# A hybrid SSD and MLA decode step: splitting the MLA output weight in an earlier stage and keeping its halves in DRAM

## The chip, the cores and the metric

The kernel runs on one core of one Trainium2 chip. The metric is the device time of one execution in microseconds, the median of several runs. The profile is that of one more execution.

## What is computed

The reference is a two-layer model: a Mamba-2 SSD mixer, then a multi-head latent attention (MLA) mixer, each behind an RMS norm and added to the residual, and a final RMS norm. A prompt of 1024 tokens and a sample group of 8 x 8 tokens go through the same weights. The sample group attends to 16 cached pages of 128 rows for each of its 8 sequences. The part that matters here is the end of the MLA layer:

```python
def mla_sample_attn(q_nope, q_pe, ckv, kpe, pool_ckv, pool_kpe, layer, page_table, w_uk, w_uv):
    q_lat = absorb(q_nope, w_uk)
    stats = latent_partial(q_lat, q_pe, ckv, kpe, causal)
    def page_step(carry, pt):
        page = latent_partial(q_lat, q_pe, pool_ckv[layer, pt], pool_kpe[layer, pt], None)
        return merge_partial(carry, page), None
    (_, l, acc), _ = lax.scan(page_step, stats, page_table.T)
    return latent_out(l, acc, w_uv)

def mla_output(o, gate, w_out):
    gated = o.reshape(b, t, MLA_WIDTH) * jax.nn.silu(gate.astype(F32))
    return jnp.einsum('bte,ed->btd', gated.astype(gate.dtype), w_out)
```

`w_out` is a float32 matrix of 1024 x 1024.

## The kernel before

Products are made from float32 operands in halves: ScalarE rounds an operand to the matmul's format (the high half), VectorE or GpSimd subtracts it from the original (the low half), and three products hi x hi, hi x lo and lo x hi are summed in PSUM. `split` is the helper. So a weight is loaded raw, cast, subtracted, and only then used.

The kernel is one program in stages. `layer_ssd` is the first layer. `mla_in` normalises, then computes the gates (`gate_block` for eight blocks of 128 columns, three pieces of tokens each; blocks 0 and 1 run inside the norm, blocks 2 to 7 as the generator `gates`), then the key-value latents (`mla_kv`, nine tiles of tokens) and the query latents (`mla_cq`). `mla_q` and `mla_heads` make the prompt's attention head by head. Inside the last head the sample group's work begins, as the generator `flow`; `mla_sample` drains the rest of it.

`flow` goes over 32 "pages": page n is an item of 512 cached rows of one sequence. A page transposes the rows of the next (`turn`, `ct`), transposes its predecessor's probabilities (`turn_p`, `pt`), makes seven score products (`scores`, `sc`), the softmax on VectorE and ScalarE (`weigh`), and twelve value products for its predecessor (`values`, `o`). Every fourth page starts a sequence with its new rows (`first_scores`, `first_values`, `first_acc`). Cached rows come by indirect loads on GpSimd's queue, four pages ahead (`load`); the rotary rows of two pages at a time come by three loads on SP's queue (`load_tk`, tile `tk`, two buffers).

Into the same pages the prompt's output projection is woven (`MlaOut.pieces`): each `next(out.fill)` is twelve products of a tile of 128 tokens with the output weight. The pieces begin at page 8 (`OUT0`), and some pages take two (`MORE`). A tile needs its attention rows (`og` from `og_d`), split into `oh` and `ol`, and its residual `h`.

The output weight has eight slices of 128 rows, in the order `WORD`. Two are loaded raw in the last head (`preload`, into `w5p`), six at the start of `mla_sample` and after (`weight`, into the three buffers that later hold `h`, named `w5r`). Pages 2 to 7 split them (`WSP` gives the page of each): one cast of 128 x 1024 on ScalarE (`w5h`), four subtractions of 128 x 256 (`w5l`) on GpSimd or VectorE in turn (`WENG`), pinned behind the page's own work by `issue_after`.

The order on TensorE and GpSimd is written out by hand in the heads and the sample stage. On ScalarE, VectorE and SP's queue a planner sorts the instructions by when they are expected to be ready; `issue_after` forces an order there. SP's queue is in order: an instruction that waits for a buffer or a result holds all behind it.

Of the kernel before, what the change touches and what calls it, by code (L numbers as in the profile page):

```python
# [51 lines left out]
MORE = (10, 12, 14, 18)  # L52
WSP = (2, 3, 4, 4, 5, 6, 6, 7)
WENG = (2, 0, 2, 0, 2, 0, 2, 0)
WORD = (0, 4, 6, 1, 2, 3, 5, 7)
# [260 lines left out]
def load_w(k, pool, src, nk, ncol, tag, bufs=3, raws=None, rbufs=2, eng=None, sub=0, late=None):  # L316
    raw = load_raw(raws or pool, nk, ncol, rbufs)
    k.nc.sync.dma_start(raw, src.rearrange("(k p) e -> p k e", p=128))
    hi = pool.tile([128, nk, ncol], F32R, tag=tag + "h", name=tag + "h", bufs=bufs)
    lo = pool.tile([128, nk, ncol], F32R, tag=tag + "l", name=tag + "l", bufs=bufs)  # L320
    if late is None:
        split(k, hi, lo, raw, eng, sub)
    else:
        late.append((hi, lo, raw))
    return hi, lo
# [635 lines left out]


def gate_block(k, wp, raws, b):
    ws = kslices(load_w(k, wp, k.I["mla_w_in"][0][:, 800 + 128 * b : 928 + 128 * b], 8, 128, "wg", 3, raws, eng=k.nc.gpsimd, sub=4), 8)
    gt = wp.tile([128, T], F32, tag="gt", name=f"gt{b}", bufs=2)

    def ev(ci, t0, n, p):
        k.nc.scalar.activation(gt[:, t0 : t0 + n], p[:, :n], AF.Silu)

    for ci in range(3):  # L970
        proj_piece(k, k.psum, ws, k.xh, k.xl, ci, ev)
        yield
    k.nc.sync.dma_start(k.g_d[b], gt)
# [13 lines left out]
def mla_in(k, right, mid):  # L987
    tc, nc, I = k.tc, k.nc, k.I
    k.g_d = k.dram.tile([8, 128, T], F32, name="g_d")
    with ExitStack() as st:  # L990
# [3 lines left out]

        rw = st.enter_context(open_pool(tc, name="rw", bufs=1))
        sg = ExitStack()
        wg = sg.enter_context(open_pool(tc, name="wpg", bufs=1))
# [8 lines left out]
        k.kvs = [k.cm.tile([128, 2, 64], F32R, name=f"kvs{x}") for x in "hl"]  # L1006
        gates = (None for b in range(2, 8) for _ in gate_block(k, wg, rw, b))
        with open_pool(tc, name="kg", bufs=1, side="right") as kg:
# [20 lines left out]
        wcq = load_cw(k, wq, rw, 0, 512, "cw")  # L1029
        mla_kv(k, sp, wkv)  # L1030
        wk.close()
# [5 lines left out]

def mla_kv(k, sp, ws):
    nc, I = k.nc, k.I
# [7 lines left out]
    for i, (t0, m) in enumerate(TILES):  # L1047
# [39 lines left out]
        if i < 8:  # L1087
            kh, kl = k.kT
            split(k, kh[64:96, t0 : t0 + m], kl[64:96, t0 : t0 + m], p[64:96, 256 : 256 + m])


# [363 lines left out]
def mla_heads(k, hd, sm, early, st):  # L1455
# [8 lines left out]
    for h in range(MH):  # L1464
# [19 lines left out]
        for t in range(12):  # L1484
            qc, jb = (0, t) if t < 4 else (1, t - 4)
            held.append((h, qc, jb, *hd.qk(h, qc, jb)))
            if t == 0:
                step(turn)
                turn = b
            while done < total * (t + 1) // 12:  # L1490
                step(units[done])
                done += 1
            if h + 1 == MH and t == 0:
                sm.preload()
            if len(held) > LEAD:
                hd.pv(*held.pop(0))
# [44 lines left out]
class Sample:  # L1541
# [28 lines left out]

    def preload(self):
        k = self.k
        self.pre = ExitStack()
        pp = self.pre.enter_context(open_pool(k.tc, name="pre4", bufs=1))
        self.wraw = {}
        for kk in WORD[:2]:
            self.wraw[kk] = pp.tile([128, D], F32, name=f"w5p{kk}")
            with k.tc.issue_after(k.lastq.ins):
                k.nc.sync.dma_start(self.wraw[kk], k.I["mla_w_out"][0][kk * 128 : kk * 128 + 128])

# [15 lines left out]
    def late_open(self, st):  # L1596
        self.pre.close()
# [10 lines left out]
    def load_tk(self, n):  # L1608
        k, nc = self.k, self.k.nc
        tk = self.ep.tile([96, 4, 256], F32R, tag="tk", name=f"tk{n}", bufs=2)  # L1610
        for j in range(3):
            src = k.kpe_d[j % 2][:, :, 128 * n : 128 * n + 256].rearrange("r c x -> c r x")
            with k.tc.issue_after(k.lastq.ins):
                nc.sync.dma_start(tk[32 * j : 32 * j + 32].bitcast(F32), src)
        for j in range(2):
            self.tk[n + j] = tk[:, :, 128 * j : 128 * j + 128]
# [12 lines left out]
    def softmax(self, name, s, n, old):  # L1629
# [4 lines left out]
        if old is None:  # L1634
            nc.vector.tensor_scalar(nm, mx, -SCALE, None, op0=ALU.mult)
        else:
            self.nmi = nc.vector.tensor_scalar(nm, mx, -SCALE, old, op0=ALU.mult, op1=ALU.min)
        P = self.sp.tile([128, n], F32, tag=f"P4{n}", name=f"P4{name}", bufs=2)
# [42 lines left out]
    def turn(self, n, c):  # L1681
# [6 lines left out]
        tl = self.ep.tile([128, 512], F32R, tag=f"cTl{c}", name=f"cTl{n}_{c}", bufs=2)  # L1688
        a = nc.scalar.copy(th, pt)
        b = nc.vector.tensor_tensor(tl, pt, th.bitcast(F32), op=ALU.subtract)  # L1690
        if self.out:
            self.out.pins = a, b
        self.cT[n, c] = (th, tl)
# [85 lines left out]
    def flow(self):  # L1779
        N = len(self.items)  # L1780
        for n in range(-1, N + 1):
# [9 lines left out]
            if t:  # L1791
                self.turn(n + 1, 1)
                yield
            parts = [WORD[WSP.index(n) + x] for x in range(WSP.count(n))] if out else []
            for kk in parts:
                out.weight_split(kk, 0)
            if 0 <= n < N:
                self.scores(n)
                self.weigh(n)
            if parts:  # L1800
                out.pins = out.pins[0], self.nmi
            for kk in parts:
                out.weight_split(kk, 1)
            if n % 4 == 3 and t:
# [19 lines left out]
            if out:  # L1824
                if n in MORE:
                    next(out.fill, None)
                if n + 1 == OUT0[0]:
                    next(out.fill)
                    self.k.nc.sync.dma_start(out.fw, self.k.I["final_norm_w"].partition_broadcast(128))
            yield  # L1830


def mla_sample(k, sm, flow):
    with ExitStack() as st:
        psum = st.enter_context(open_pool(k.tc, name="ps4", bufs=1, space=PS))
        out = MlaOut(k, st, psum)
        sm.open(st, psum, out)
        out.raw = sm.wraw
        for kk in WORD[2:5]:
            out.weight(kk)  # L1840
        out.fill = fill = out.pieces(range(8))
        next(fill)
        for _ in flow:
            if not hasattr(sm, "accT") and not any(kk in out.raw for kk in WORD[:2]):
                sm.late_open(st)
        last = None
# [11 lines left out]
class MlaOut:  # L1858
    def __init__(self, k, st, psum):
        tc, nc, I = k.tc, k.nc, k.I  # L1860
# [3 lines left out]
        self.fw = sp.tile([128, D], F32, name="fw")  # L1864
        self.raw = {}
        self.ws = [[self.wp.tile([128, D], F32R, name=f"w5{x}{kk}", bufs=1) for x in "hl"] for kk in range(8)]

    def weight(self, kk):
        k, nc, wp = self.k, self.k.nc, self.wp
        self.raw[kk] = self.sp.tile([128, D], F32, tag="h5", name=f"w5r{kk}", bufs=3)  # L1870
        WQ(nc).dma_start(self.raw[kk], k.I["mla_w_out"][0][kk * 128 : kk * 128 + 128])

    def weight_split(self, kk, half):
        hi, lo = self.ws[kk]
        raw = self.raw[kk]
        nc, x = self.k.nc, WENG[WORD.index(kk)]
        if not half:
            with self.k.tc.issue_after(self.pins[0].ins):
                nc.scalar.copy(hi, raw)
        for a in range(2 * half, 2 * half + 2):  # L1880
            s = slice(256 * a, 256 * a + 256)
            with self.k.tc.issue_after(self.pins[1].ins):
                (nc.gpsimd if x & 2 else nc.vector).tensor_tensor(lo[:, s], raw[:, s], hi[:, s].bitcast(F32),
                                                                  op=ALU.subtract)
        if half:
            del self.raw[kk]
            if 2 <= WORD.index(kk) < 5:
                self.weight(WORD[WORD.index(kk) + 3])

    def pieces(self, tiles, src=None):  # L1890
        k, nc, sp, ws = self.k, self.k.nc, self.sp, self.ws

        def load(i):
# [4 lines left out]
            if i < 8:  # L1898
                g = sp.tile([128, 8, 128], F32, tag="og5", name=f"og5{i}", bufs=2)
                nc.sync.dma_start(g, k.og_d[:, :, t0 : t0 + m].rearrange("b p t -> p b t"))  # L1900
            return oh[:, :, :m], oh[:, :, 64:] if m == 64 else ol, g, oh
# [7 lines left out]
        for n, i in enumerate(tiles):  # L1909
            t0, m = TILES[i]  # L1910
            oh, ol, _, o2 = queue.pop(0)
            h = sp.tile([128, D], F32, tag="h5", name=f"h5{i}", bufs=3)
            nc.sync.dma_start(h[:m], k.h_d[t0 : t0 + m])
            if n + 1 < len(tiles):
# [5 lines left out]
            for hf, c in enumerate(cs):  # L1920
# [3 lines left out]
                for j, _ in enumerate(mm_tok(nc, p, m, nw, [  # L1924
                        (oh[:, kk], ol[:, kk], o2[:, kk], ws[kk][0][:, c], ws[kk][1][:, c]) for kk in WORD])):
                    if j == (7 if src else 11) and nw == 512:
# [138 lines left out]
```

## Time and profile before

| what | value |
|---|---|
| median of 3 runs | 1947.31 us (1943.63 to 1948.73) |
| profiled execution | 1942.63 us |
| its span, first to last instruction | 1940.9 us |
| granted TensorE clock, mean | 0.995 |
| busy share PE, DVE, ACT, POOL | 98%, 61%, 57%, 44% |
| DMA moved | 202.02 MB, mean 104 GB/s |

PE is TensorE's products, DVE is VectorE, ACT is ScalarE, POOL is GpSimd; a trailing q means the engine's sequencer or queue (SPq issues most of the DMAs). Times are microseconds from the start of the span. A row of a timeline has start, length, engine, source line, operation, `out<-in`, shapes, and in brackets how long the engine stood idle before it and who released it. In the table by windows come, for each stretch, its length, the busy time of each engine with its instructions in brackets, the granted clock as a share of full speed, the busy share of the DMA engines and GB/s.

### The profile page before, as it was taken

The page shows a single profiled execution, that of the slowest core. Times are in us where ns is not written, and L with a number is a line of the kernel's source. Part 1 is how long each engine was busy: PE and PEld are TensorE (multiplying, and loading weights), DVE is VectorE, ACT ScalarE, POOL GpSimd, SP SyncE. Part 2 cuts the span into 40 slices and gives each one's busy share as a digit, 9 for nine tenths or more (in the row PEclk, how much of TensorE's full clock was granted, in tenths as well). Part 3 has the DMA queues.
Part 4 walks back from the last instruction along what each step waited for, and adds up shares of the span by engine and source line. Part 5 has one row for each costly group of instructions (what it writes and reads, how often), then busy time and mean ns, then how long its engine had stood idle before and what let it go on. Part 6 is the DMA issues. An engine that isn't in the chain of part 4 may idle for free.

```text
span 1940.9 us, 33581 instructions
## 1 busy us (share of the span) xinstructions
PE 1896.4 (98%) x12023; PEld 1731.9 (89%) x12023; DVE 1191.3 (61%) x2447; ACT 1110.6 (57%) x2535; POOL 844.3 (44%) x1122
## 2 busy tenths in 40 slices
PE   9999999999999999899999999999999999999998
PEld 7999999999999999788787998898888888778887
DVE  5557565756665666765533104466787878676674
ACT  6466676666667676743214314335777777855552
POOL 2447455555655555444003213203443434774551
PEclk9999999999999999999999999999999999999999
DMA  5123323332333332553533333132111112654441
GB/s 165 50 72 87 92 84 98 82 110 82 93 89 93 83 99 66 189 180 133 197 124 109 134 141 91 64 109 89 55 52 41 52 41 59 205 177 154 155 128 39
DMA packets 181087, 202.02 MB, mean 104 GB/s; under 512 B 18828, under 2 KB 147608, under 8 KB 180536
## 3 DMA queue, kind: packets, MB, share of 16 engines
q1 hardware_dynamic: 175864, 180.08, 30.3%
q0 software_dynamic: 4976, 19.66, 3.0%
q8 instruction: 95, 1.56, 0.3%
q14 instruction: 72, 0.59, 0.1%
q10 hardware_dynamic: 80, 0.13, 0.0%
HBM read 146.52 MB, written 53.28 MB: 103 GB/s over the span
## 4 chain that ended last, share of the span: by engine, by line
PE 85%; ACT 4%; DVE 3%; DMA 3%; POOL 2%; issue 1%; SPq 0%; POOLq 0%; DVEq 0%; ACTq 0%
PE pj L86 21%; PE pz L98 8%; PE pq L98 6%; PE pob L98 5%; PE p L98 5%; PE poa L98 5%; PE py L635 2%; PE sc L86 2%; PE o L86 2%; PE sc L1365 2%; PE o L1428 2%; PE o L1430 2%; PE st L1397 2%; PE st L1398 2%; PE st L1399 2%; PE o L1429 2%
## 5 line engine op out<-in xcount | busy, mean ns | idle before, releaser
L86 PE MATMUL pj<-xh,wih 128*128 128x384 f32 (+1 forms) x768 | 254.7, 336 | 0.5 <-ACT raw L512 0.3
L86 PE MATMUL pj<-xl,wih 128*128 128x384 f32 (+1 forms) x768 | 254.1, 331 | 0.0
L86 PE MATMUL pj<-xh,wil 128*128 128x384 f32 (+1 forms) x768 | 253.6, 330 | 0.0
L1411 POOL TENSOR_TENSOR tl<-P,th 128x384 fp32r<-128x384 f32 (+1 forms) x96 | 90.6, 944 | 232.5 <-ACT P L1409 190.9
L526 DVE SCALAR_TENSOR_TENSOR acc<-raw,vec,acc 128x1112 f32<-128x1112 f32 x96 | 141.6, 1476 | 26.5 <-ACT acc L522 25.5
L86 PEld LDWEIGHTS pj<-xh,wih 128*128 128x128 f32 x768 | 144.3, 189 | 2.2 <-ACT xh L273 0.7
L86 PEld LDWEIGHTS pj<-xl,wih 128*128 128x128 f32 x768 | 144.9, 189 | 1.0
L86 PEld LDWEIGHTS pj<-xh,wil 128*128 128x128 f32 x768 | 144.7, 188 | 0.4
L98 PE MATMUL pz<-wih,xh 128*128 128x256 f32 x504 | 142.8, 287 | 0.5 <-ACT z L567 0.5
L98 PE MATMUL pz<-wil,xh 128*128 128x256 f32 (+1 forms) x504 | 140.2, 284 | 0.0
L1408 ACT ACTIVATE th<-st 128x512 fp32r<-128x512 f32 x192 | 94.6, 493 | 65.9 <-PE st L1404 50.3
L98 PE MATMUL pz<-wih,xl 128*128 128x256 f32 x448 | 128.2, 286 | 0.0
L630 ACT ACTIVATE M<-M,tok 128x128 f32<-128x128 f32 (+1 forms) x288 | 90.9, 386 | 64.2 <-DVE M L627 63.8
L1701 POOL TENSOR_TENSOR kvl<-pgr,kvh 128x256 fp32r<-128x256 f32 x128 | 97.6, 789 | 57.4 <-ACT kvh L1699 57.0
L98 PEld LDWEIGHTS pz<-wih,xh 128*128 128x128 f32 x504 | 95.9, 190 | 1.3 <-ACT z L567 0.9
L1409 ACT ACTIVATE P<-st 128x512 f32<-128x512 f32 x192 | 93.5, 487 | 0.0
L98 PEld LDWEIGHTS pz<-wil,xh 128*128 128x128 f32 (+1 forms) x504 | 92.7, 184 | 0.7
L627 DVE TENSOR_TENSOR M<-M,negu 128x512 f32<-128x512 f32 x64 | 50.6, 790 | 67.2 <-DMA M<-acs_d 67.1
L133 DVE TENSOR_TENSOR wil<-wraw,wih 128x512 fp32r<-128x512 f32 x88 | 72.2, 828 | 25.8 <-ACT wih L127 22.7
L98 PEld LDWEIGHTS pz<-wih,xl 128*128 128x128 f32 x448 | 85.3, 190 | 0.1
L613 POOL TENSOR_TENSOR xdd<-xsT,tok 128x256 f32<-128x256 f32 x64 | 50.2, 784 | 80.7 <-ACT xsT L599 80.3
L1411 DVE TENSOR_TENSOR tl<-P,th 128x512 fp32r<-128x512 f32 x96 | 70.8, 737 | 18.9 <-ACT P L1409 18.0
(832 smaller groups left out, 6308.3 us busy)
## 6 DMA issues: line engine op xcount, KB each, us to landing
wraw<-in_ssd_w_in SPq DMA_DIRECT2D x92, 256.0 KB
M<-acs_d SPq DMA_DIRECT2D x64, 256.0 KB
s<-in_state_ssm SPq DMA_DIRECT2D x32, 256.0 KB
y_d<-y SPq DMA_DIRECT2D x64, 128.0 KB
out_s_ssm<-s SPq DMA_DIRECT2D x32, 256.0 KB
wraw<-in_ssd_w_out SPq DMA_DIRECT2D x12, 512.0 KB
q_d<-qt SPq DMA_DIRECT2D x32, 192.0 KB
qp<-q_d SPq DMA_DIRECT2D x8, 768.0 KB
```

Of the source, the lines that this page charges most:

```text
L86: nc.tensor.matmul(out, a, b, start=(i == 0), stop=(i == n - 1))
L98: nc.tensor.matmul(o, a, b, start=(j == 0), stop=(j == len(ops) - 1))
L133: return (eng or nc.vector).tensor_tensor(lo, src, hi.bitcast(F32), op=ALU.subtract)
L526: last = nc.vector.scalar_tensor_tensor(acc, raw[:, j : j + n], k.convw[j][:, blk : blk + 1], acc, op0=ALU.mult, op1=ALU.add)
L613: nc.gpsimd.tensor_tensor(v3(xdd), v3(xsT), hb(2), op=ALU.mult)
L627: nc.vector.tensor_tensor(M[:m, :, :m], M[:m, :, :m], (k.negs if smp else k.negu)[:m, :m].unsqueeze(1).to_broadcast([m, 4, m]), op=ALU.add)
L630: nc.scalar.activation(M[:m, h, :m], M[:m, h, :m], AF.Exp, bias=tk[:, 0, 4 * g + h : 4 * g + h + 1])
L635: nc.tensor.matmul(py[:m, h * 64 : h * 64 + 64], M[:m, h, :m], xsT[:m, h * 64 : h * 64 + 64], start=True, stop=True)
L1408: nc.scalar.activation(th[:, :n], ps[:, :n], AF.Exp, scale=SCALE)
L1409: nc.scalar.activation(P[:, :n], ps[:, :n], AF.Exp, scale=SCALE)
L1411: eng.tensor_tensor(tl[:, :n], P[:, :n], th[:, :n].bitcast(F32), op=ALU.subtract)
L1701: nc.gpsimd.tensor_tensor(rl[:, j], raw[:, j], rh[:, j].bitcast(F32), op=ALU.subtract)
```

## The change

The output weight's split leaves the pages. A generator `stage_out` handles it in sixteen steps of half a slice (128 x 512): load raw, cast on ScalarE, subtract in place on VectorE, store both halves to a DRAM tensor `w5_d`. Nine of the steps are taken among the pieces of gate blocks 2 to 7, the rest behind the latent tiles of `mla_kv`. Each raw load is put behind the newest weight load of `load_w`.

In the last head `preload` fetches two slices in halves (1 MB each) that stay where they are; pages 2 to 7 fetch one slice each, put behind the newest rotary-row load on SP's queue. The loads of attention rows, residuals and the final norm's weight are put behind the newest rotary rows too. The first attention tile is loaded at page 6 and split at page 7; before, its load was asked for at the start of `mla_sample`. The accumulator tiles of `late_open` no longer wait for the preloaded slices' memory.

```diff
-WSP = (2, 3, 4, 4, 5, 6, 6, 7)
-WENG = (2, 0, 2, 0, 2, 0, 2, 0)
+NPW = 2
+WSP = (2, 3, 4, 5, 6, 7)
@@ load_w
-    k.nc.sync.dma_start(raw, src.rearrange("(k p) e -> p k e", p=128))
+    k.lastload = k.nc.sync.dma_start(raw, src.rearrange("(k p) e -> p k e", p=128))
@@
+def stage_out(k, pool):
+    nc = k.nc
+    k.w5_d = k.dram.tile([8, 128, 2, D], F32, name="w5_d")
+    for n in range(16):
+        kk, s = WORD[n // 2], slice(512 * (n % 2), 512 * (n % 2) + 512)
+        t = pool.tile([128, 2, 512], F32, tag="w5s", name=f"w5s{n}", bufs=3)
+        with k.tc.issue_after(k.lastload.ins):
+            nc.sync.dma_start(t[:, 1], k.I["mla_w_out"][0][kk * 128 : kk * 128 + 128, s])
+        nc.scalar.copy(t[:, 0].bitcast(F32R), t[:, 1])
+        nc.vector.tensor_tensor(t[:, 1].bitcast(F32R), t[:, 1], t[:, 0], op=ALU.subtract)
+        nc.sync.dma_start(k.w5_d[kk][:, :, s], t)
+        yield
@@ mla_in
         rw = st.enter_context(open_pool(tc, name="rw", bufs=1))
+        stage = stage_out(k, st.enter_context(open_pool(tc, name="w5s", bufs=1)))
...
-        gates = (None for b in range(2, 8) for _ in gate_block(k, wg, rw, b))
+        def gate_steps():
+            for b in range(2, 8):
+                for ci, _ in enumerate(gate_block(k, wg, rw, b)):
+                    if (3 * b + ci) % 2:
+                        next(stage, None)
+                    yield
+        gates = gate_steps()
...
-        mla_kv(k, sp, wkv)
+        mla_kv(k, sp, wkv, stage)
@@ mla_kv, at the end of each tile
+        next(stage, None)
@@ Sample.preload
-        for kk in WORD[:2]:
-            self.wraw[kk] = pp.tile([128, D], F32, name=f"w5p{kk}")
+        for kk in WORD[:NPW]:
+            self.ws[kk] = pp.tile([128, 2, D], F32R, name=f"w5{kk}")
             with k.tc.issue_after(k.lastq.ins):
-                k.nc.sync.dma_start(self.wraw[kk], k.I["mla_w_out"][0][kk * 128 : kk * 128 + 128])
+                k.nc.sync.dma_start(self.ws[kk].bitcast(F32), k.w5_d[kk])
@@ Sample.load_tk
-                nc.sync.dma_start(tk[32 * j : 32 * j + 32].bitcast(F32), src)
+                self.lasttk = nc.sync.dma_start(tk[32 * j : 32 * j + 32].bitcast(F32), src)
@@ Sample.flow
-            parts = [WORD[WSP.index(n) + x] for x in range(WSP.count(n))] if out else []
-            for kk in parts:
-                out.weight_split(kk, 0)
+            if out and n >= 0:
+                out.weights(n)
             if 0 <= n < N:
                 self.scores(n)
                 self.weigh(n)
-            if parts:
-                out.pins = out.pins[0], self.nmi
-            for kk in parts:
-                out.weight_split(kk, 1)
...
+                if n + 2 == OUT0[0]:
+                    next(out.fill)
                 if n + 1 == OUT0[0]:
                     next(out.fill)
-                    self.k.nc.sync.dma_start(out.fw, self.k.I["final_norm_w"].partition_broadcast(128))
+                    with self.k.tc.issue_after(self.lasttk.ins):
+                        self.k.nc.sync.dma_start(out.fw, self.k.I["final_norm_w"].partition_broadcast(128))
@@ mla_sample
         sm.open(st, psum, out)
-        out.raw = sm.wraw
-        for kk in WORD[2:5]:
-            out.weight(kk)
+        sm.late_open(st)
+        k.sm = sm
         out.fill = fill = out.pieces(range(8))
-        next(fill)
...
@@ MlaOut
+    def weights(self, n):
+        k = self.k
+        for x in range(WSP.count(n)):
+            kk = WORD[NPW + WSP.index(n) + x]
+            with k.tc.issue_after(k.sm.lasttk.ins):
+                WQ(k.nc).dma_start(self.ws[kk].bitcast(F32), k.w5_d[kk])
@@ MlaOut.pieces
-                nc.sync.dma_start(g, k.og_d[:, :, t0 : t0 + m].rearrange("b p t -> p b t"))
+                with k.tc.issue_after(k.sm.lasttk.ins):
+                    nc.sync.dma_start(g, k.og_d[:, :, t0 : t0 + m].rearrange("b p t -> p b t"))
...
-            nc.sync.dma_start(h[:m], k.h_d[t0 : t0 + m])
+            with k.tc.issue_after(k.sm.lasttk.ins):
+                nc.sync.dma_start(h[:m], k.h_d[t0 : t0 + m])
```

More of the change, by code (lines that the diff above doesn't have):

```diff
@@ L1035, in mla_in, with mla_kv @@
         mla_cq(k, sp, wcq)
-def mla_kv(k, sp, ws):
+def mla_kv(k, sp, ws, stage):
     nc, I = k.nc, k.I
@@ L1493, in mla_heads @@
             if h + 1 == MH and t == 0:
-                sm.preload()
+                sm.preload(st)
             if len(held) > LEAD:
@@ L1569, in pt, with preload @@
         return self.psum.tile([128, 512], F32, tag=tag, name=name, bufs=bufs)
-    def preload(self):
+    def preload(self, st):
         k = self.k
-        self.pre = ExitStack()
-        pp = self.pre.enter_context(open_pool(k.tc, name="pre4", bufs=1))
-        self.wraw = {}
-        for kk in WORD[:2]:
-            self.wraw[kk] = pp.tile([128, D], F32, name=f"w5p{kk}")
+        pp = st.enter_context(open_pool(k.tc, name="pre4", bufs=1))
+        self.ws = {}
+        for kk in WORD[:NPW]:
+            self.ws[kk] = pp.tile([128, 2, D], F32R, name=f"w5{kk}")
             with k.tc.issue_after(k.lastq.ins):
-                k.nc.sync.dma_start(self.wraw[kk], k.I["mla_w_out"][0][kk * 128 : kk * 128 + 128])
+                k.nc.sync.dma_start(self.ws[kk].bitcast(F32), k.w5_d[kk])
     def load_cn(self, b):
@@ L1596, in late_open @@
     def late_open(self, st):
-        self.pre.close()
         ap = st.enter_context(open_pool(self.k.tc, name="ap4", bufs=1))
@@ L1636, in softmax @@
         else:
-            self.nmi = nc.vector.tensor_scalar(nm, mx, -SCALE, old, op0=ALU.mult, op1=ALU.min)
+            nc.vector.tensor_scalar(nm, mx, -SCALE, old, op0=ALU.mult, op1=ALU.min)
         P = self.sp.tile([128, n], F32, tag=f"P4{n}", name=f"P4{name}", bufs=2)
@@ L1688, in turn @@
         tl = self.ep.tile([128, 512], F32R, tag=f"cTl{c}", name=f"cTl{n}_{c}", bufs=2)
[L1689 to L1692, printed above, removed]
+        split(k, th, tl, pt)
         self.cT[n, c] = (th, tl)
@@ L1835, in mla_sample @@
         psum = st.enter_context(open_pool(k.tc, name="ps4", bufs=1, space=PS))
-        out = MlaOut(k, st, psum)
+        out = MlaOut(k, st, psum, sm)
         sm.open(st, psum, out)
-        out.raw = sm.wraw
-        for kk in WORD[2:5]:
-            out.weight(kk)
+        sm.late_open(st)
+        k.sm = sm
         out.fill = fill = out.pieces(range(8))
-        next(fill)
-        for _ in flow:
-            if not hasattr(sm, "accT") and not any(kk in out.raw for kk in WORD[:2]):
-                sm.late_open(st)
+        drain(flow)
         last = None
@@ L1858, with __init__ @@
 class MlaOut:
-    def __init__(self, k, st, psum):
+    def __init__(self, k, st, psum, sm):
         tc, nc, I = k.tc, k.nc, k.I
@@ L1864, in __init__ @@
         self.fw = sp.tile([128, D], F32, name="fw")
[L1865 to L1888, printed above, removed]
+        self.ws = dict(sm.ws)
+        for kk in WORD[NPW:]:
+            self.ws[kk] = self.wp.tile([128, 2, D], F32R, name=f"w5{kk}", bufs=1)
+    def weights(self, n):
[4 more added lines that the diff above has]
+                WQ(k.nc).dma_start(self.ws[kk].bitcast(F32), k.w5_d[kk])
     def pieces(self, tiles, src=None):
@@ L1924, in pieces @@
                 for j, _ in enumerate(mm_tok(nc, p, m, nw, [
-                        (oh[:, kk], ol[:, kk], o2[:, kk], ws[kk][0][:, c], ws[kk][1][:, c]) for kk in WORD])):
+                        (oh[:, kk], ol[:, kk], o2[:, kk], ws[kk][:, 0, c], ws[kk][:, 1, c]) for kk in WORD])):
                     if j == (7 if src else 11) and nw == 512:
```

## The prediction, made before the changed kernel was run

> **What bounds the kernel now.** I read the page first (PE is busy for 98% of the span, and the chain that ended last is 85% PE), so time can only come from stretches in which PE is not full. The table by windows finds the one that the change touches.
>
> ```profile
> core 0: us, PE busy (x) PEld busy (x) DVE busy (x) ACT busy (x) POOL busy (x), PEclk, DMA share, GB/s
> 1081.86:1158.25 76.39, 75.22 (x468) 74.79 (x468) 5.44 (x8) 17.54 (x33) 15.99 (x23) 1.00 0.36 131
> 1158.25:1197.20 38.95, 38.95 (x270) 36.99 (x269) 14.56 (x78) 13.18 (x40) 15.44 (x24) 1.00 0.30 88
> 1653.00:1660.00 7.00, 7.00 (x48) 6.28 (x47) 4.26 (x9) 6.57 (x17) 5.64 (x7) 1.00 0.96 321
> 1675.25:1718.69 43.44, 34.91 (x209) 29.72 (x207) 38.42 (x74) 30.86 (x57) 36.25 (x45) 0.88 0.81 251
> 1679.50:1693.50 14.00, 9.54 (x60) 8.37 (x61) 11.26 (x25) 11.88 (x22) 8.58 (x11) 0.90 1.01 307
> 1690.00:1700.00 10.00, 7.91 (x30) 6.65 (x31) 10.00 (x17) 8.39 (x16) 6.83 (x8) 0.54 0.94 272
> 1718.69:1907.00 188.31, 188.31 (x1117) 163.03 (x1116) 118.86 (x262) 101.65 (x221) 98.37 (x124) 1.00 0.42 135
> ```
>
> The stretch 1675.25 to 1718.69 holds the sample pages 2 to 7, where the output weight is split today. PE is busy for 34.91 of 43.44 us and DVE for 38.42. From page 8 on the output pieces fill PE (188.31 of 188.31 us): what those pages take is PE's own work, and the change leaves it alone. So the question is how much sooner page 8 starts. The timeline of PE gives each page's first score product, and the wait list of PE for the same stretch says what held it.
>
> ```profile
> 1675.25 0.48 PE L86 MATMUL sc<-cTh,qlh 128*128 128x512 f32 x1
> 1680.60 0.48 PE L86 MATMUL sc<-cTh,qlh 128*128 128x512 f32 x1
> 1686.97 0.48 PE L86 MATMUL sc<-cTh,qlh 128*128 128x512 f32 x1
> 1698.58 0.78 PE L86 MATMUL sc<-cTh,qlh 128*128 128x512 f32 x1
> 1705.72 0.48 PE L86 MATMUL sc<-cTh,qlh 128*128 128x512 f32 x1
> 1712.38 0.48 PE L86 MATMUL sc<-cTh,qlh 128*128 128x512 f32 x1
> 1718.69 0.48 PE L86 MATMUL sc<-cTh,qlh 128*128 128x512 f32 x1
> 1720.43 0.48 PE L98 MATMUL p<-w5h,oh 128*128 128x512 f32 x1
> ```
>
> ```profile
> engine line waited for: us in total, times, longest us
> PE pt L1728 <- ACT P L1640: 3.5, 4, 1.9
> PE pt41n L1667 <- ACT P41n L1640: 3.2, 1, 3.2
> PE o L86 <- DVE pTl L133: 1.7, 2, 1.0
> ```
>
> The page periods are 5.35, 6.37, 11.61, 7.14, 6.66 and 6.31 us. PE never waits for a DMA here: it waits 8.4 us in all for ACT and DVE, most of it for the softmax. Why those were late shows in their timelines:
>
> ```profile
> 1684.32 0.16 DVE L1659 TENSOR_TENSOR sn<-sc41n,smk 128x8 f32<-128x8 f32 x1
> 1685.11 3.86 DVE L1883 TENSOR_TENSOR w5l<-w5p,w5h 128x256 fp32r<-128x256 f32 x4
> 1688.89 0.15 DVE L1632 TENSOR_REDUCE mx41n<-sn 128x1 f32<-128x8 f32 x1
> ...
> 1689.74 2.00 ACT L1879 CAST w5h<-w5r 128x1024 fp32r<-128x1024 f32 x2
> 1691.64 0.31 ACT L1640 ACTIVATE P41n<-sn,nm41n 128x8 f32<-128x8 f32 x1
> ...
> 1692.09 0.38 PE L1667 MATMUL pt41n<-ident,P41n 128*8 128x128 f32 x1 [3.25 <-ACT P41n L1640]
> ```
>
> The new rows' scores were ready at 1684.32; their maximum came after 3.86 us of weight split on DVE, their exponential after 2.00 us of weight split on ACT. PE stood 3.25 us for it and then ran at a granted clock of 0.54. (The chain gives 7.24 us here to a rotary-row load, but PE's list has no such wait, and that load serves pages 6 and 7.) So the weight split is what ends last.
>
> **The change, part by part.** Removed from pages 2 to 7, by the groups of instructions of that stretch:
>
> ```profile
> L1883 DVE TENSOR_TENSOR w5l<-w5r,w5h 128x256 fp32r<-128x256 f32 x12 | 9.7, 852 | 0.0
> L131 DVE TENSOR_TENSOR ol<-og,oh 128x256 fp32r<-128x256 f32 x8 | 5.0, 679 | 0.0
> L1883 DVE TENSOR_TENSOR w5l<-w5p,w5h 128x256 fp32r<-128x256 f32 x4 | 3.9, 1021 | 0.0
> ...
> L1879 ACT CAST w5h<-w5r 128x1024 fp32r<-128x1024 f32 x6 | 6.2, 1056 | 0.2 <-DMA w5r<-in_mla_w_out 0.2
> L1879 ACT CAST w5h<-w5p 128x1024 fp32r<-128x1024 f32 x2 | 2.1, 1052 | 0.0
> L127 ACT CAST oh<-og 128x1024 fp32r<-128x1024 f32 x2 | 2.1, 1047 | 0.8 <-DMA og<-og_d 0.8
> ```
>
> That is 13.6 us of DVE and 8.3 us of ACT, besides POOL's half of the subtractions. DVE keeps 38.42 - 13.6 - 5.0 = 19.8 us, 3.3 a page, and then fits under a page. What is late next is the page's own loop (scores, maximum, exponential, transpose). Its period without weight work is best read from pages 2 to 3, 5.35 us, in which only the first weight cast is mixed. Six of them are 32.1 us. To this come PE's products for new rows, which that period lacks:
>
> ```profile
> 1725.24 0.62 PE o42n L1676 x2
> ...
> 1745.66 0.68 PE sc43n L86 x7
> ```
>
> Two score groups and one value group fall into the six pages: 2 x 0.68 + 0.62 = 2.0 us. The split of the first attention tile stays, now in page 7 (the second moves behind page 8, into pages that PE bounds). Its four DVE pieces are 4 x 0.679 = 2.7 us, against 5.35 - 3.3 = 2.05 us that DVE has free, so between 0.65 and 2.7 us show; I take 1.2. Together 35.3 us for 43.44: **8.1 us gained**. The ends: bound by PE alone, the six pages need the 34.91 us less what the mean clock of 0.88 added, 34.91 x 0.12 = 4.2 us, so 30.7, a gain of 12.7; at the 6.37 us of the next page six take 38.2, with the 1.2 a gain of 4.
>
> Added in the gate and latent stage: 16 loads, 16 casts of 512 columns on ACT, 16 subtractions of 512 on DVE, 16 stores. Nearest rows of that size:
>
> ```profile
> 1161.82 0.61 ACT L127 CAST cw0h<-wraw 128x512 fp32r<-128x512 f32 x1
> 1212.53 0.68 DVE L133 TENSOR_TENSOR cql<-cqs,cqh 128x512 fp32r<-128x512 f32 x1
> 1641.45 4.07 DVE L1411 TENSOR_TENSOR tl<-P,th 128x512 fp32r<-128x512 f32 x1
> ```
>
> 16 x (0.61 + 0.68) = 20.6 us if nothing hid them. PE's projections hide them: nine steps lie among gate pieces, where ACT is busy for 17.54 and DVE for 5.44 of 76.39 us, seven among the latent tiles (13.18 and 14.56 of 38.95 us, PE full). A gate evacuation behind a cast is at most 0.61 us late, and there are two buffers. In the latent tiles a subtraction beside POOL could last 4.07 us as it did at 1641.45, and seven times the surplus of 3.4 us would be 24 us on a chain that PE covers with query products. Below nothing is excluded, as no PE work goes from this stage. I take 0.4 us. On SP a store that waits for its subtraction has the gate and query weight loads queued behind it; gates are loaded a block ahead (76.39 / 6 = 12.7 us), so a few us of waiting are covered.
>
> Traffic, by the tiles' shapes in the code: the gate and latent stage gets 4.2 MB of raw loads and 8.4 MB of stores, 12.6 MB over 115 us or 109 GB/s, on top of 131 and 88 GB/s; DMA moved 307 and 321 GB/s when it was full. Pages 2 to 7 read 6.3 MB of slices for 3.1 MB of raw weight, which is tighter. What opens SP's queue there, before:
>
> ```profile
> 1671.26 0.27 PE L1404 MATMUL st<-mr 128*128 128x128 f32 x1
> ...
> 1678.92 0.45 SPq L1442 DMA_DIRECT2D og_d<-og  x1
> 1679.47 1.50 SPq L1871 DMA_DIRECT2D w5r<-in_mla_w_out  x3
> ```
>
> Then attention tiles, norm weight and residuals came in as early as their buffers allowed. After the change they come behind rotary rows that are issued once older scores have freed their buffer; in the later pages each is issued a tile ahead, two pages or more, so only the first can be late. Until the first attention tile has landed there pass five slices (5.24 MB), two groups of rotary rows (0.79), that tile (0.52) and six pages (3.15): 9.70 MB, at 307 GB/s 31.6 us. The slices go into buffers that the last head frees with its last score product at 1671.26, 7.6 us ahead of the store that holds SP until 1678.92. If they start then, the tile lands about 1703, and 1.05 + 2.7 us later its halves stand, ahead of page 8 (about 1710.6): nothing is lost. I take this. The Trainium skill ("DMA: Bandwidth & Descriptors", Specifications) puts a core's HBM limit at about 358 GB/s; by it the transfer would take an estimated 27.1 us and the tile would be in time from either start. The rows show 307 and 321 in full stretches, and the sum goes by those.
>
> Sum: -8.1 + 0.4 = -7.7 us. The profiled execution took 1942.63 us (span 1940.9 and 1.7 around it), so its like would be 1934.9. The median of the three runs, 1947.31, is 4.7 above it; with the same 7.7 off I predict **1939.6**.
>
> **The rivals.**
> *DMA takes the place of the split.* The slices start only behind the store, at 1679.5. At 321 to 307 GB/s the tile lands at 1709.7 to 1711.1, the first piece starts 3.75 us later, 1713.5 to 1714.8 instead of 1720.43: 5.6 to 6.9 us sooner, of which up to 4.2 go again where the wait for it drops the clock as at 1692. About 3 us stay: 1944. For it: DMA at 1.01 from 1679.5 on. Against: the slices' buffers are free earlier.
> *Slower.* The same start, and the rate stays at the stretch's mean of 251 GB/s, since small rows and indirect pages mix with the slices. The tile lands at 1679.5 + 38.6 = 1718.1, the first piece starts at 1721.9, 1.4 later than now, and PE, which came to it at about 1712, has stood some 10 us; a clock lost as at 1690 costs 4.2 more. With 0.4 in the gates that is +6.0: 1953.3. It decides below 9.70 MB / 33.0 us = 294 GB/s, where landing, halves and half clock together eat the gain. For it: six slices of double size. Against: 307 and 321 were reached with such rows in the mix. The Trainium skill ("TensorE: Matmul & The Clock Gate", Part 1) has the clock back after about 3.4 us of busy PE; by that the half clock would cost an estimated 1.7, not 4.2. The row at 1690 to 1700 (0.54) speaks for the longer one.
> *The staging is not hidden.* Query weights come late behind stores on SP, latent tiles wait for subtractions beside POOL: 5 of the 20.6 us show, the gain falls to 3: 1944 as well.
>
> **How the numbers follow.** About 0.3%, 5.8 us, is what a measurement of this kernel can tell from no change. The forecast, 1939.6 (own range 1934 to 1943), has 0.65; the two rivals that leave about 3 us 0.20 together; the slower one 0.15. A little of the forecast's range lies within 0.3%, and a little of the rivals' beyond it on the fast side; they offset. The range reaches from the PE bound (1947.31 - 12.7 + 0.4 = 1935.0, with 1 us for the runs' own scatter) past no change to 1949.5, leaving out most of the slower case.
>
> **What would show it.** In the changed profile, the first score product of page 2 to that of page 8 takes about 35 us, PE's list there has no wait over 2 us, and no slice of clock is near 0.5. The gate stage keeps PE full and grows by under 1 us. Slices are issued ahead of the last store of the heads. I am wrong if PE waits at page 8 for the attention tile's halves, if page periods stay above 6.4 us without weight work (then the softmax loop was the bound), or if PE has new gaps before 1200 us.

## The result and the profile after

The changed kernel took 1954.09 us in the median (1949.87 to 1958.02, 14 runs), the kernel before 1945.03 us (1940.62 to 1949.32) on the same chip. The ratio is 1.0042, with a 95% interval of 1.0033 to 1.0052: slower by some 8 us, where 7.7 us less was forecast. The profiled execution took 1953.21 us, its span 1951.4. PE's busy time did not change (1896.2 us, before 1896.4): all that was lost is time in which PE stood.

Four marks on PE say where the 10.5 us between the two spans lie: the first transpose of a latent tile (`ckp`), the first score product of page 2, the first output piece and the end. To the first mark the changed kernel is 1.0 us ahead (1164.1 for 1165.1), from there to page 2 it takes 4.3 more (514.4 for 510.1), from page 2 to the first piece 5.1 more (50.3 for 45.2), from there to the end 2.1 more (222.6 for 220.5).

The table by windows of the changed kernel (columns as in the prediction):

```profile
1080.00:1160.00 80.00, 78.92 (x496) 78.49 (x495) 9.52 (x15) 20.96 (x38) 16.43 (x23) 1.00 0.55 202
1160.00:1200.00 40.00, 38.00 (x256) 35.27 (x256) 18.51 (x84) 16.50 (x45) 15.45 (x24) 1.00 0.61 192
1678.54:1727.06 48.52, 32.76 (x208) 28.05 (x206) 24.16 (x57) 23.44 (x51) 24.16 (x31) 0.86 0.74 253
1684.33:1714.73 30.40, 20.09 (x133) 17.06 (x131) 13.18 (x30) 12.84 (x29) 16.10 (x21) 0.92 1.03 350
1727.06:1907.00 179.94, 178.69 (x1064) 154.25 (x1063) 113.93 (x251) 96.87 (x211) 91.39 (x115) 1.00 0.48 152
```

The gates keep PE as full as before:

```profile
1080.00:1160.00 80.00, 78.83 (x494) 78.40 (x493) 6.68 (x13) 17.98 (x33) 16.61 (x24) 1.00 0.35 128
```

The latent tiles lose 2.00 us of 40. Pages 2 to 7, the third row, take 48.52 us instead of 43.44, though DVE's work there fell from 38.42 to 24.16 and PE's by 2.15. PE's timeline, with the pages' first score products, shows one step among them:

```profile
1678.54 0.48 PE L86 MATMUL sc<-cTh,qlh 128*128 128x512 f32 x1
...
1700.56 0.48 PE L86 MATMUL sc<-cTh,qlh 128*128 128x512 f32 x1
...
1719.22 1.12 PE L1747 MATMUL pt<-ident,P 128*128 128x128 f32 x4 [14.38 <-ACT P L1662]
...
1720.84 0.78 PE L86 MATMUL sc<-cTh,qlh 128*128 128x512 f32 x1
...
1727.06 0.48 PE L86 MATMUL sc<-cTh,qlh 128*128 128x512 f32 x1
...
1728.81 0.48 PE L98 MATMUL p<-w,oh 128*128 128x512 f32 x1
```

Pages 2 to 5 take 22.02 us, 5.5 each. Then PE stands 14.38 us, in page 7, for page 6's exponential (L1662). Why that was late is in the timelines of ACT and DVE, and the reason for those in that of SP's queue:

```profile
1701.63 0.60 ACT L127 CAST cTh<-ct 128x512 fp32r<-128x512 f32 x1
1714.73 1.04 ACT L127 CAST oh<-og 128x1024 fp32r<-128x1024 f32 x1 [12.50 <-DMA og<-og_d]
...
1718.39 0.69 ACT L1662 ACTIVATE P<-sc,nm 128x512 f32<-128x512 f32 x1 [2.13 <-DVE nm L1659]
```

```profile
1715.81 1.43 DVE L131 TENSOR_TENSOR ol<-og,oh 128x256 fp32r<-128x256 f32 x4 [12.63 <-ACT oh L127]
1717.16 0.68 DVE L1654 TENSOR_REDUCE mx<-sc 128x1 f32<-128x512 f32 x1
```

```profile
1683.69 0.45 SPq L1466 DMA_DIRECT2D og_d<-og  x1
1684.33 1.41 SPq L1887 DMA_DIRECT2D w<-w_d  x3
...
1686.55 6.53 SPq L1636 DMA_DIRECT2D tk<-kpe_dh  x1
...
1694.35 0.90 SPq L1887 DMA_DIRECT2D w<-w_d  x2
...
1699.27 0.38 SPq L1900 DMA_DIRECT2D og<-og_d  x1
```

Each engine runs its instructions in order. The planner put the cast of the first attention tile, which the code has at the end of page 7, ahead of page 6's exponential, as if the tile were there. It was asked for at 1699.27, behind five slices in a DMA that was full (1.03, 350 GB/s), and had landed at 1714.73, when its cast starts. ACT stood 12.50 us for it, DVE 12.63 behind ACT, and the softmax of the page behind both.

### The profile page after: what moved, and what is told of

Read it like the earlier page. It is cut to its first block, busy times and chain, and to the rows that moved or that the text cites. A ratio compares the mean times of both kernels' runs of the same rounds, so it can differ in the third digit from the quotient of the medians.

```text
span 1951.4 us, 33639 instructions
## 1 busy us (share of the span) xinstructions
PE 1896.2 (97%) x12023; PEld 1729.2 (89%) x12023; DVE 1186.1 (61%) x2447; ACT 1110.6 (57%) x2543; POOL 828.4 (42%) x1106
## 4 chain that ended last, share of the span: by engine, by line
PE 77%; DMA 6%; ACT 5%; POOL 4%; DVE 4%; issue 4%; SPq 0%; POOLq 0%; DVEq 0%; ACTq 0%
PE pj L86 19%; PE pz L98 8%; PE pob L98 5%; PE pq L98 5%; PE poa L98 5%; PE p L98 3%; PE py L635 2%; PE sc L1389 2%; PE o L1452 2%; DMA M<-acs_d 2%; PE o L1454 2%; PE st L1421 2%; PE st L1422 2%; PE st L1423 2%; PE o L1453 2%
## 5 line engine op out<-in xcount | busy, mean ns | idle before, releaser
L98 PE MATMUL p<-w,oh 128*128 128x512 f32 (+3 forms) x304 | 88.7, 385 | 0.6 <-DVE h L1929 0.6
```

Source lines behind the costliest of these rows:

```text
L98: nc.tensor.matmul(o, a, b, start=(j == 0), stop=(j == len(ops) - 1))
```

## The experiments

Theory: the loss is in the order of the instructions on ACT and DVE, which wait for a late tile ahead of the page's softmax; a smaller part is the staging in the latent tiles. Rivals: the slices' doubled bytes cost whatever the order; the staging is the whole loss or none; or it is the late start of the slices that decides.

**e1_stage_only.** The kernel before, with `stage_out` and its calls added and nothing else.

> The kernel before, with the staging of the change added in the gate and latent stages (raw halves loaded, split, stored to DRAM) and nothing read back: pages 2 to 7 split the weight as they did. Theory (two losses): the latent tiles lose about 2 us of PE and the pages start about 3.3 us later, and nothing else moves: 2.5 to 3.5 us slower than the kernel before, ratio 1.0013 to 1.0018. Rival 'the staging is hidden, the whole loss is in the pages': within 0.5 us, ratio 1.000. Rival 'staging is the main loss': 6 us or more, ratio above 1.003.

Measured: ratio 1.0023 (1.0012 to 1.0035), 4 us. Page 2 starts at 1677.75 us instead of 1675.25; the latent tiles take 42.4 us from first to last transpose, before 39.7, and from the first to page 2 513.9, before 510.1. The pages themselves are unchanged, 45.2 us to the first piece. So the staging costs about 4 us, somewhat above the expected 2.5 to 3.5 (whose ratios lie within the interval), and is not the whole loss.

**e2_split_pinned.** The changed kernel with one split moved.

```diff
-        split(k, *queue[0][:3], parts=4 if tiles[0] == 0 else 0)
+        with k.tc.issue_after(k.sm.lastexp.ins) if tiles[0] == 0 else ExitStack():
+            split(k, *queue[0][:3], parts=4 if tiles[0] == 0 else 0)
```

`lastexp` is the newest page exponential. ACT's program differs from the changed one's in the place of this cast and of one cast of a page's rows (`cTh`), which stood behind it; SP's loads have the same order.

> The changed kernel, with one thing moved: the cast of the first attention tile on ACT and its subtractions on DVE are issued behind page 7's exponential, where the code has them, not ahead of page 6's. All loads stay where they are. Theory (order on ACT and DVE): the tile still lands near 1714.7 us, PE's 14.4 us wait for page 6's exponential goes, page 7 starts near 1706, and the first output piece starts when the halves stand, at about 1718.5 instead of 1729.0: 10 us faster than the changed kernel, and some 2 us faster than the kernel before (ratio 0.999). Rival 'bytes' (the slices of double size saturate DMA and hold up whatever comes behind them): the first piece stays near 1729 and the time at ratio 1.004; PE then waits for a DMA instead.

Measured: 1.0040 (1.0027 to 1.0053), the ratio of the rival and not the 0.999 of the theory. The trace is not the rival's: the first wait is gone, page 7 starts at 1705.70, page 8 at 1711.02, and the first piece at 1715.09, which the rival had near 1729. (The profiled execution is the fastest of five, 1948.64 us with a median of 1952.40, so it shows less of the loss than the ratio.) But PE then stands at the second tile:

```profile
1726.01 1.04 ACT L127 CAST oh<-og 128x1024 fp32r<-128x1024 f32 x1 [9.39 <-DMA og<-og_d]
1726.96 0.68 ACT L1662 ACTIVATE P<-sc,nm 128x512 f32<-128x512 f32 x1
```

```profile
1727.79 1.12 PE L1747 MATMUL pt<-ident,P 128*128 128x128 f32 x4 [5.62 <-ACT P L1662]
```

The same line-up one tile on: the second tile's cast ahead of page 8's exponential, its load asked for at 1712.04. In the changed kernel the first wait had covered it, since it held the pages back: PE stood 0.3 us there.

**e3_tile_early.** As e2, and the first tile's load ahead of all slices (`next(fill)` at the start of `mla_sample`, no `issue_after` for that load).

> As the run before (split of the first attention tile behind page 7's exponential), and the load of that tile is issued ahead of all slices instead of behind five of them. Theory (place in the queue): the tile lands near 1690 us, no engine waits for it, and the first piece starts when page 8 is reached or the last slice has landed, 1713 to 1716 us: 5 to 7 us faster than the kernel before (ratio 0.9965 to 0.9975). Rival 'bytes': the slices themselves and the rotary rows come late, PE waits for a slice or for the rows, and the first piece starts at 1720 or later: ratio 1.000 to 1.004.

Measured: 1.0032 (1.0021 to 1.0043), the rival's ratio, but not by its mechanism. Nothing waits for the first tile, and page 8 starts at 1712.93; the second tile's cast waits as in e2:

```profile
1729.06 1.11 PE L1747 MATMUL pt<-ident,P 128*128 128x128 f32 x4 [7.82 <-ACT P L1662]
```

**e4_stage_gates.** All staging steps between gate pieces.

```diff
-                    if (3 * b + ci) % 2:
-                        next(stage, None)
+                    next(stage, None)
...
-        mla_kv(k, sp, wkv, stage)
+        mla_kv(k, sp, wkv, iter(()))
```

> The changed kernel with all 16 staging steps between pieces of gate blocks 2 to 7 and none in the latent tiles. Theory: gate pieces cover the steps, the latent tiles keep PE full, and the pages start some 3 us sooner; the 14.4 us wait at the first attention tile stays: 2 to 3.5 us faster than the changed kernel, ratio to the kernel before 1.0025 to 1.0033. Rival 'the steps cost the same wherever they stand' (their DVE and ACT time, or their traffic): ratio 1.004 as the changed kernel has it.

Measured: 1.0033 (1.0021 to 1.0045), which tells it from neither. The trace does: the latent tiles take 39.7 us again, but the gate stage, from the norm's last transpose to the first latent transpose, takes 89.6 us for 86.6. What the tiles won the gates lost.

**e5_pins.** As e2, with the other tiles' splits pinned behind `lastexp` as well.

> The changed kernel with the cast and subtractions of every attention tile issued behind the exponential of the page in which the code has them, so not only the first tile's as in the run before. Loads stay as they are: late, behind slices and rotary rows. Theory (ACT and DVE wait in order for a late tile, and the page's exponential stands behind): the second wait, 5.6 us at page 8's exponential in the run with the first tile alone, goes as well; page 8 starts near 1711, the first piece near 1715, and from there PE is full: about 5 us faster than the kernel before, ratio 0.996 to 0.998. Rival 'the loads are too late for the pieces themselves': PE waits for the second tile's halves or for residual rows inside the pieces, and the ratio stays at 1.002 to 1.004.

Measured: 0.9964 (0.9950 to 0.9979), as expected: faster than the kernel before, and by 1.0042 / 0.9964 some 0.8% faster than the changed one, with the same loads, bytes and staging. Its pages by windows, and what is left of waiting there:

```profile
1681.54:1713.84 32.30, 30.50 (x208) 26.42 (x207) 22.27 (x53) 21.54 (x49) 23.41 (x30) 1.00 0.92 308
```

```profile
1718.31 1.22 PE L98 MATMUL p<-w,oh 128*128 128x512 f32 x2 [1.90 <-ACT oh L127]
```

Six pages in 32.30 us with PE busy for 30.50, at the full clock. The tile still lands late (at 1717.2, 35.7 us after page 2 begins; 36.2 in the changed kernel) but only its own piece waits for it. In the profiled executions the stretch from page 2 to the end takes 259.2 us, in the changed kernel 272.9 and before 265.7.

**e6_loads_free** and **e7_loads_free_pins.** One part of the change undone: attention tiles, residuals and norm weight are loaded as early as buffers allow, e6 with the splits where the planner puts them, e7 with the pins of e5.

```diff
-                with k.tc.issue_after(k.sm.lasttk.ins):
-                    nc.sync.dma_start(g, k.og_d[...])
+                nc.sync.dma_start(g, k.og_d[...])
```

and so for `h` and `fw`, with `next(fill)` at the start of `mla_sample`.

> The changed kernel with one part undone: attention tiles, residuals and norm weight are loaded as early as their buffers allow, as in the kernel before; slices alone stay behind rotary rows. The splits stand where the scheduler puts them. Theory: the first two tiles land ahead of the slices, near 1690, no exponential waits behind a cast, and the last slice lands near 1716: the first piece starts at 1714 to 1717, ratio 0.996 to 0.998. Rival 'the doubled slices cost whatever order they come in': the slices are now the late ones, PE waits for them at page 8 until 1722 or later, ratio 1.001 or more.

> Both of the last two: loads of the output stage early, splits behind the exponential of their page. Theory: as either alone, and within 1.5 us of the better; ratio 0.995 to 0.998. If only one of them works (early tiles collide with page loads, or pinned splits come too late), it differs from the better one by more than 2 us.

Measured: 1.0027 (1.0016 to 1.0038) and 1.0001 (0.9986 to 1.0016). Both expectations of the theory fell. In e6 an exponential, now page 3's, again stands behind the first tile's cast, ahead of which ACT was idle for 3.12 us, and PE waits for it:

```profile
1696.85 1.11 PE L1747 MATMUL pt<-ident,P 128*128 128x128 f32 x4 [3.12 <-ACT P L1662]
```

Besides, the early loads fill the queue ahead of the rotary rows; e7's SP queue and PE:

```profile
1689.75 10.61 SPq L1636 DMA_DIRECT2D tk<-kpe_dh  x1
```

```profile
1709.84 0.76 PE L86 MATMUL sc<-tk,qpr 96*128 96x512 f32 x1 [5.48 <-DMA tk<-kpe_dh]
```

SP is held for 10.61 us in issuing one rotary load, and PE stands 5.48 us for the rows (3.90 in e6). So the change's rule that output loads go behind rotary rows is good: with the pins it is worth 0.9964 against 1.0001. It needs the pins, since it makes the tiles late.

**e8_hi_only.** The six late slices bring only their high half, which is used for the low one too, so that part of the result is left out and PE's work is the same.

> The changed kernel, with only the high half of the six late slices read (0.5 MB each instead of 1 MB), and the high half used in place of the low one in the output products, so that PE's work is the same and the output is not the reference's. Everything keeps its order. Theory: 3.1 MB less ahead of or beside the first tile are 9 us at 350 GB/s; it lands near 1706, the wait for page 6's exponential falls from 14.4 to about 5 us, and the kernel is 8 to 12 us faster than the changed one, ratio 0.998 to 1.000. Rival 'it is the place in the queue alone, not the bytes': the tile lands as late as before, ratio 1.004.

Measured: 1.0005 (0.9990 to 1.0019). The wait for page 6's exponential is 4.41 us, close to the expected 5; the time came down by 7 us, a little less than expected. Bytes and order both enter: the bytes set when the tile lands, the order who waits for it. With the order mended (e5) the full bytes cost little.

**e9_store_pool** and **e10_pins_store.** The last head's last store goes to POOL's queue, in e9 on the changed kernel, in e10 on e5.

```diff
-        nc.sync.dma_start(k.og_d[pr, pj, cs], og[pj])
+        (nc.gpsimd if h == MH - 1 and qc else nc.sync).dma_start(k.og_d[pr, pj, cs], og[pj])
```

> The changed kernel; only the last head's last store of the attention output is issued from POOL's queue instead of SP's, so that the slices no longer stand behind it. Tests the forecast's assumption that the slices' buffers are free when the last head's scores are done. If they are: the slices are issued near 1678 instead of 1684, the first tile lands some 6 us sooner, the wait of 14.4 us for page 6's exponential falls to about 8, and the kernel is 5 to 8 us faster than the changed one: ratio 1.000 to 1.0015. If something else holds the buffers: slices near 1684 as before, wait 14 us, ratio 1.004.

> The run with all splits pinned behind their page's exponential (0.9964), with the last store on POOL's queue as well. If the earlier start is worth something behind the pins, the tile lands some 6 us sooner, its cast no longer waits at page 8 (3.4 us there), and the first piece starts with page 8's scores: 2 to 4 us faster, ratio 0.9945 to 0.9955. If the rotary rows or pages now meet the slices earlier, the pages lose as much: ratio 0.996 to 0.998.

Measured: 1.0013 (1.0001 to 1.0025) and 0.9967 (0.9951 to 0.9984). In e9:

```profile
1680.29 0.27 PE L1454 MATMUL o<-tl,Vh 128*128 128x128 f32 x1
```

```profile
1680.52 1.74 SPq L1887 DMA_DIRECT2D w<-w_d  x3
```

```profile
1712.72 1.11 PE L1747 MATMUL pt<-ident,P 128*128 128x128 f32 x4 [5.81 <-ACT P L1662]
```

The slices start right behind the head's last value product, 1.1 us ahead of page 2 where they started 5.8 behind it in the changed kernel, and the wait falls to 5.81 us. Behind the pins it gives nothing that can be measured, against the expected 0.9945 to 0.9955: the late tile no longer held the pages.

**e11_pins_query** and **e12_all.** e5 with the seven staging steps of the latent tiles moved behind the query latents' tiles; then e11 and e10 together.

> The run with all splits pinned, and the seven staging steps of the latent tiles moved behind the tiles of the query latent that follow, where PE was full, ACT busy for 22 and DVE for 23 of 50 us. Theory (three steps bunched beside the latent tiles' own short chain cost 2.4 us of PE there): the latent tiles take 39.7 us again, and the kernel is 2 to 2.5 us faster: ratio 0.995. Rival 'a step costs the same wherever it stands' (as when all 16 went into the gates): the query tiles or the heads' preparation lose it, ratio 0.996 to 0.997.

> All three edits: splits pinned, last store on POOL's queue, seven staging steps in the query tiles. If their gains add up: 0.9925 to 0.9945; if only the pins count: 0.996 to 0.997.

Measured: 0.9963 (0.9948 to 0.9978) and 0.9965 (0.9950 to 0.9980). In e11 the latent tiles take 39.7 us again, but the stretch from the first latent transpose to page 2 is 0.8 us shorter than in e5 (512.4 for 513.2), not 2.4. In e12's profile PE stands 4.96 us for a page of cached rows beside the slices. Only the pins give a gain that can be measured; e5 is the simplest of four versions that cannot be told apart and that beat both kernels.

## Why the prediction was wrong

**The page loop without weight work: right in kind, too small.** Free of the wait, six pages took 31.9 us in e2 and 32.3 in e5, where the forecast had 35.3: 11.1 to 11.6 us gained, not 8.1. The mis-sized term is the 3.2 us added to six periods of 5.35 (32.1 us). The period itself was nearly right: page 2 takes 5.35 us in e2 and e5 too, where no weight cast is left. But the new rows hardly lengthened the pages, and the first tile's split fell behind page 8, as its tile came late. PE's own work in the six pages, 30.50 us in e5, is what the forecast had as its bound, 30.7. That split work on DVE and ACT bound these pages is shown: e7, whose output loads come as early as before, does pages 2 to 5 in 21.3 us, the kernel before in 30.5. Of e5's 11.1 us, 8.4 are left at the first piece, which waits for the late tile (36.8 us from page 2, before 45.2).

**Start of the slices: wrong, and worth a part of the loss.** The forecast let them start at the last score product, ahead of the head's store. They started at 1684.33, behind the store, as its first rival had it. Nor are the buffers free that early: with the store out of the way (e9) the slices start at 1680.52, as the last value product ends. Of the size of it: the changed kernel's DMA moved 10.64 MB from the first slice to the landing, for 9.70 forecast, in 30.40 us for 31.6. With the early start the ratio falls from 1.0042 to 1.0013, but the wait without pins is still 5.81 us; with pins the start makes no difference that can be measured (e10).

**Who waits for the tile: the step that failed.** The forecast and its two rivals about DMA let the late tile delay only its own piece, 3.75 us after landing. By that step a landing at 1714.73 would have given a first piece at 1718.5, sooner than before. The cast and subtractions stood two pages earlier on ACT and DVE, ahead of a softmax, so the lateness fell on PE's page loop: 14.38 us. The slower rival had the sign and a total (+6.0) near the result, but put it on a rate below 294 GB/s; the rate was 350, and its cause is not what happened. Moving that order alone (e5) takes the kernel from 1.0042 to 0.9964, which is 0.36% below before. There the tile lands as late after the start of page 2, so it is the order that decides. That 0.36% is near the forecast 0.4% is luck: the pages gave some 3 us more than forecast, and the staging took some 3 us more. Nor is all of it located: in the profiled executions e5 is 3.4 us ahead of the kernel before from the first latent transpose to the end, by the medians' ratio 7.

**Half clock.** After the wait the granted clock was 0.50, then 0.89 in the slice from 1723 to 1724:

```profile
1722.00:1723.00 1.00, 1.00 (x4) 0.81 (x3) 0.59 (x1) 0.00 (x0) 1.00 (x2) 0.50 0.00 0
1723.00:1724.00 1.00, 1.00 (x8) 0.82 (x7) 0.17 (x1) 0.00 (x0) 0.41 (x2) 0.89 0.00 0
```

PE resumed at 1719.22, so the clock was back after about 4.0 us of work, and half speed cost 2.0 us. The pages' account closes with it: 48.52 - 14.38 - 2.0 = 32.1 us. For this wait the rivals' 4.2 was too high, but no wait has a fixed price. In the kernel before PE resumed at 1692.09, was then busy throughout, and had half the clock until about 1701, some 9 us, which cost about 4.5:

```profile
1700.00:1701.00 1.00, 1.00 (x4) 0.80 (x3) 1.00 (x4) 0.55 (x1) 0.96 (x1) 0.50 0.00 0
1701.00:1702.00 1.00, 0.83 (x5) 0.54 (x3) 1.00 (x3) 0.00 (x0) 0.97 (x3) 0.96 0.45 133
```

In e8 it was 9.4 us, from 1716.33. What decides between 4 and 9 us is not shown. The Trainium skill ("TensorE: Matmul & The Clock Gate", Part 1) has the clock back after about 3.4 us of busy TensorE. The estimate of 1.7 from it was the nearer one for the changed kernel; the kernel before and e8 do not agree with it.

**Staging: mis-sized by ten times.** Forecast 0.4 us with bounds of nothing to 20.6, measured 4.3 in the trace and 4 by e1. Of it 2.8 us lie in the latent tiles (42.5 for 39.7) and the rest in the query stages behind them. That PE covers the latent tiles' chain with query products was wrong:

```profile
PE ckp L1106 <- DVE ckv L1082: 2.0, 2, 1.6
```

```profile
1179.82 2.12 DVE L972 TENSOR_TENSOR w5s<-w5s 128x512 fp32r<-128x512 f32 x3 [1.44 <-ACT w5s L971]
1183.18 0.48 DVE L1082 SCALAR_TENSOR_TENSOR ckv<-pk,rr,kvw 128x256 f32<-128x256 f32 x1 [0.17 <-POOL rr L224]
```

The loads landed in bursts of three, and three subtractions ran in one block ahead of a tile's own short chain. The gates kept PE full (78.92 of 80, before 78.83), as forecast, until e4 put all steps there. Moving the steps does not save the whole price. From the first query product (`pq<-wqh`) to the heads' first `st` the changed kernel takes 91.6 us, the kernel before 89.6, and e4 and e11, whose latent tiles lose nothing, still 91.7 and 91.5, although e4 has no staging step there. Their wait lists have new waits of 1.6 to 1.7 us, for the evacuation of the queries (`qt`) and for their reload (`qp`). What makes these late, and what costs e4 its 3.0 us in the gates, stays open.

**After page 8: nearly right.** The forecast left these pages alone; the changed kernel takes 2.1 us more from the first piece to the end, with 1.3 us of idle PE between 1727.06 and 1907. In e5 and e10, whose PE is full from 1800 to 1900, the same stretch is as long (222.4 and 222.6), and PE is busy longer behind the first piece for as many products (213.7 us in e10, 212.4 before, 1265 each); why stays open. What separates e5 from the changed kernel lies before it.

The wrong signs named at the end of the forecast were partly the right ones: PE had a long wait, but at page 7's transpose for an exponential, not at page 8 for the halves; the periods of pages 2 to 5 fell to 5.1 to 6.1 us; the gap before 1200 us was there.

## What to carry to other kernels

When a load is made later, look not at its consumer's consumer but at what stands behind its first reader on that reader's in-order engine; a planner that believes in early data will put a cast ahead of a softmax. Pin such a reader behind the work that must not wait, and late data then delay only themselves. In a full DMA, order loads by when they are needed: putting the output loads behind the rotary rows was worth 0.4% once the pins were there, and brought no gain without them.

## What the runs showed of the hardware

SP, whose queue issues a load in 0.3 to 0.5 us, was held for 6.53 us (the changed kernel) to 10.61 us (e7) by the issue of one 128 KB load behind slices of 1 MB; behind slices of half that size (e8) it was 1.97 us. So large loads still under way can hold SP itself, and with it all that stands behind in the queue, not only the transfers. A core alone got 350 GB/s over 30.4 us, and 360 in e10's pages:

```profile
1683.65:1716.45 32.80, 30.76 (x209) 26.37 (x207) 22.71 (x53) 22.03 (x50) 25.08 (x32) 1.00 1.03 360
```

That is above the 307 to 321 of the forecast's rows. A full DMA has no one rate: at about the same share the changed kernel moved 418 GB/s for 8 us, and e8 294 GB/s from its first late slice to the cast of the first tile (22.5 us).

```profile
1688.00:1696.00 8.00, 7.87 (x55) 6.60 (x55) 4.86 (x15) 6.38 (x16) 5.39 (x7) 1.00 1.01 418
```

The Trainium skill ("DMA: Bandwidth & Descriptors", Specifications) has about 358 GB/s as a core's HBM limit. The means over 30 us lie near it, but the stretch of 418 GB/s is above it, so these runs do not show it as a limit. With the DMA at a share of 1.03, PE still lost only 2 of 32.8 us in e10's pages.
